# Two heads at a time in the row halves of TensorE, in the second block's two attentions of a fused two-block network

## The chip, the cores and the metric

The kernel runs on one core of one Trainium2 chip. The metric is the device time of one execution in microseconds (us), taken as the median over runs. TensorE (PE in the profile, PEld its weight loads) multiplies into PSUM, which has eight banks of 2 KB in each of 128 partitions; VectorE (DVE), ScalarE (ACT) and GpSimd (POOL) work on its results; SyncE (SP) starts the weight transfers.

## The reference, cut to what matters

One batch, 256 tokens, 1024 channels, all in float32. A first block (three mixers and a feed-forward) is followed by a second block, whose mixer has two attentions; a mixture of 32 experts follows and its weights are most of what is read from memory. Only the two attentions are changed:

```python
def hybrid_mixer(h, ...):
    z = h @ w_in                                   # fq fk fv ff dq dk dv and two gates
    log_f = log_sigmoid(ff + b_fgate)              # 8 heads
    o_a = fox_attention(fq, fk, fv, log_f)         # 8 heads of 64
    ob = diff_attention(q1, q2, k1, k2, vh, lam, slopes)   # 4 heads, two maps of 64 each, values of 128
    ...
def fox_attention(q, k, v, log_f):
    F = cumsum(log_f)
    s = q k^T * scale + F[query] - F[key]          # causal mask, softmax
    return softmax(s) v
def diff_attention(...):
    s1 = q1 k1^T * scale + bias;  s2 = q2 k2^T * scale + bias   # bias: -slope * distance, mask by chunks of 64
    return (softmax(s1) - lam * softmax(s2)) v
```

The softmax leaves F[query] out, since it is the same for a whole row.

## The kernel before, in words

Everything is one program on one core. Tokens are two tiles t of 128; a score tile is 128 queries by 128 keys for t=0 and by 256 keys for t=1, and so 384 numbers in a row for a head. In float32 a product is issued as two passes, which is why one call in the code shows as `x2` in the trace. The large projections are split into a high and a low part (`wh`/`wl`, `xT2h`/`xT2l`), and are three passes each: the tiles `acc_c` (q and k projections by `lin_chan`, 256 columns a pass) and `acc_t` (v and the gates by `lin_tok`, 512 columns a pass) are those.

The second block (`block2`) is a set of Python generators: `fk`, `fq`, `fv`, `dk`, `dq`, `dv`, `g0` to `g3` (projections and gates), `fg` (`forget`, the sums of log_f), `f0` to `f3` (`fox(b)`, heads 2b and 2b+1), `d0` to `d3` (`diff(h)`), and the projections of the outputs after them. The list `ORDER2` says in which order their pieces are written, each `yield` ending a piece; a scheduler then fixes the order of each engine's queue, by which instruction is ready when. So the small matmuls of the attentions stand between the passes of `acc_c` and `acc_t` on PE.

Names used below: `fsc` and `dsc` are the score tiles, `fptr` and `dptr` the transposed probabilities, `fPT` their copy in SBUF, `fpo` and `dpo` the outputs of the two attentions, `pF` the sums of log_f and `nFh`/`nFl` its high and low parts, `sel8` a pattern of ones and zeros that adds one row of them to all queries, `cb` constants in bf16 (the causal mask; for `dsc` distances and slopes). `attn_probs` takes the maximum of a row (`prm`, DVE), the exponential with its sum (`pr`, ACT) and a reciprocal (`prs`, DVE). At the start of the block `ptx` transposes the tokens `xt` to `xT2h`/`xT2l`, and `prb` spreads the norm's factor, which comes from `ssum`, `rmsa`, `rrms` and `dg`, over a tile.

In `fox` one head after another has its scores in one bank of the tag `mn`: for each t a product of 64 rows, two sums of 8 rows each, and the mask. In `diff` each (t, map) has a bank of `mn` of its own, one product of 64 rows and one bias matmul of 128 rows. q and k of two heads (or of two maps) lie in the partitions 0 to 63 and 64 to 127 of one tile; a product of 64 rows uses one half of the array's rows. `fpo` has its two heads in the partitions 0 to 63 and 64 to 127 of one bank, so that each matmul uses one half of the array's columns.

PSUM banks come from a pool `ps` that lives from the first block to the end of the second: three for `acc`, two for `mg`, three for `mn`. After the second block other pools take their place.

Of the kernel before, what the change touches and what calls it, by code (L numbers as in the profile page):

```python
# [18 lines left out]
P = 128  # L19
# [13 lines left out]
ORDER2 = ("fk x x fq fk fk fk fk lam fq fq fv fq fq fq x fg fg fk fv fv fv fv fv dk f1 f1 dk f2 f1 f2 f1 dq f0 "  # L33
# [133 lines left out]
def fused_kernel(ctx, tc, I, out, dbg=None):  # L167
# [28 lines left out]
    acc, mx, mg, mn = psum("acc"), psum("mx"), psum("mg"), psum("mn")  # L196
# [209 lines left out]
    with ExitStack() as st:  # L406
# [6 lines left out]
        with banks("ps", acc=3, mg=2, mn=3):  # L413
            acc(), mg()
            block1(K)
            later_inputs()
            ffn(K)
            K.st8.close()
            dump("x1", xt)
            block2(K)  # L420
            dump("x2", xt)
# [858 lines left out]
def block2(K):  # L1280
    nc, tc, I = K.nc, K.tc, K.I
    V, S, G, PE = K.V, K.S, K.G, K.PE
    C, CB, PR, idn, idb, mg, mn, acc, dump = K.C, K.CB, K.PR, K.idn, K.idb, K.mg, K.mn, K.acc, K.dump
    xt, sp, xT = K.xt, K.sp, K.x2
    with ExitStack() as st:
# [21 lines left out]
        nFh = we.tile([8, T], F32R, name="nFh")  # L1307
        nFl = we.tile([8, T], F32R, name="nFl")
        sel8 = we.tile([8, 8], F32R, name="sel8")
# [30 lines left out]
        def forget():  # L1340
# [4 lines left out]
            V.tensor_copy(sel8, idn[:8, :8])  # L1345
# [3 lines left out]
            pF = mn((8, T), name="pF")  # L1349
            PE.matmul(pF, sf[:, 0], C("UT"), start=True, stop=False)  # L1350
            PE.matmul(pF[:, P:], sf[:, 1], C("UT")[:, :P], start=False, stop=True)
            S.activation(nFh, pF, AF.Copy)
            V.tensor_tensor(nFl, pF, nFh.bitcast(F32), op=OP.subtract)
# [19 lines left out]

        def fox(b):
            po = None
            for i in range(2):
                h, hh = 2 * b + i, slice(64 * i, 64 * i + 64)
                sc = mn((P, 384), name="fsc")
                for t in range(2):
                    nk = P * (t + 1)  # L1380
                    o = sc[:, t * P:t * P + nk]
                    PE.matmul(o, fqT[hh, b, t * P:t * P + P], fkT[hh, b, :nk], start=t == 0, stop=False, skip_group_check=True)
                    PE.matmul(o, sel8[:, h:h + 1].to_broadcast([8, P]), nFh[:, :nk], start=False, stop=False, skip_group_check=True)
                    PE.matmul(o, sel8[:, h:h + 1].to_broadcast([8, P]), nFl[:, :nk], start=False, stop=False, skip_group_check=True)
                    PE.matmul(o[:, nk - P:], idb, CB("CM"), start=False, stop=t == 1, skip_group_check=True)
                yield
                ptr = mg((P, 384), name="fptr")
                for t in range(2):
                    nk = P * (t + 1)
                    pr, sm = attn_probs(K, we, sc, t * P, nk, "pr")  # L1390
                    G.tensor_scalar(pr[:, :nk], pr[:, :nk], sm, 1.0, op0=OP.mult, op1=OP.mult)
                    transpose_probs(pr, t, ptr)
                PT = we.tile([P, 384], F32, name="fPT", tag="PT2", bufs=2)
                S.activation(PT, ptr, AF.Copy)
                yield
                if not i:
                    po = mn((P, T), name="fpo")
                PE.matmul(po[hh], fv[:, 0, h * 64:h * 64 + 64], PT[:, :T], start=True, stop=False)
                PE.matmul(po[hh, P:], fv[:, 1, h * 64:h * 64 + 64], PT[:, T:], start=False, stop=True)
# [6 lines left out]
        def diff(h):  # L1406
            ptr = mg((P, 384), name="dptr")
            for t in range(2):
                nk = P * (t + 1)
                e = []  # L1410
                for i in range(2):
                    hh = slice(64 * i, 64 * i + 64)
# [80 lines left out]
        def mix(n):  # L1493
            ns = slice(n * 512, n * 512 + 512)
            y = gate[:, :, :D]
            if not ys:
                ys.append(K.Rows(y, None, "yT2", (K.s8a, K.s8a)))
# [563 lines left out]
```

## Time and profile before

| | |
|---|---|
| time, median of 3 runs | 1055.98 us (1054.99 to 1058.1) |
| the profiled execution: its time | 1054.65 us |
| its span in the trace | 1052.8 us |
| mean granted TensorE clock | 0.991 |
| PE busy | 1029.7 us (98%) |
| DVE, ACT, POOL busy | 448.4 us (43%), 290.1 us (28%), 207.1 us (20%) |
| moved by DMA | 292.57 MB, mean 278 GB/s |

The span is what the engines' records cover; 1.85 us of the execution lie outside it. The second block's part treated here runs from about 370 to 540 us in the span, and the experts from about 600 us to the end.

### The profile page before, as it was taken

What the parts mean: (1) busy time and instruction counts of PE and PEld (TensorE: products, weight loads), DVE (VectorE), ACT (ScalarE), POOL (GpSimd) and SP (SyncE); (2) the same over time, 40 slices, a digit from 0 to 9 for tenths busy, and PEclk for the clock granted to TensorE, in tenths of its full rate; (3) what the DMA queues carried; (4) which work ended last, traced back from release to release, by engine and by line L of the source; (5) the groups of instructions that cost most, each with busy time, mean ns of one, the idle gap of its engine ahead of it and who ended that gap; (6) DMA issues with size and microseconds to landing.
All of it is one profiled execution on the core that took longest, in us unless ns stands there. A gap on an engine that the chain in (4) does not pass through costs nothing. (4 is left out here: it accounts for less than half of the span.)

```text
span 1052.8 us, 16017 instructions
## 1 busy us (share of the span) xinstructions
PE 1029.7 (98%) x6373; PEld 719.0 (68%) x6373; DVE 448.4 (43%) x929; ACT 290.1 (28%) x628; POOL 207.1 (20%) x299
## 2 busy tenths in 40 slices
PE   7999999999999999999999999999999999999995
PEld 6789777988899897876788644445444555555553
DVE  4676768666555744346677411111111111111112
ACT  4554344333223453234443211110011110110012
POOL 3662262222222243332334200000000000000000
PEclk9999999999999999899999999999999999999998
DMA  9552287556555553243668899999999999999993
GB/s 347 156 156 81 78 204 275 177 193 199 185 176 188 165 178 123 100 141 128 216 244 332 321 377 422 421 421 419 420 421 421 420 419 421 419 421 420 418 390 106
DMA packets 83596, 292.57 MB, mean 278 GB/s; under 512 B 11648, under 2 KB 27840, under 8 KB 60480
## 3 DMA queue, kind: packets, MB, share of 16 engines
q1 hardware_dynamic: 82368, 289.68, 73.5%
q10 hardware_dynamic: 1152, 1.86, 0.5%
q8 instruction: 51, 0.84, 0.3%
q14 instruction: 25, 0.20, 0.1%
HBM read 289.87 MB, written 1.64 MB: 277 GB/s over the span
## 5 line engine op out<-in xcount | busy, mean ns | idle before, releaser
L1733 PE MATMUL ph<-w,xe 128*64 128x512 f32 x1024 | 224.9, 593 | 0.0
L1733 PEld LDWEIGHTS ph<-w,xe 128*64 128x64 f32 x1024 | 85.7, 137 | 128.4 <-issue 126.2
L1733 PE MATMUL po_e<-w,gT 128*64 128x512 f32 (+1 forms) x528 | 115.1, 584 | 0.7 <-ACT gT L1833 0.7
L294 DVE TENSOR_TENSOR wl<-ffn,wh 128x512 fp32r<-128x512 f32 (+1 forms) x100 | 85.2, 855 | 62.4 <-ACT wh L293 31.4
L308 POOL TENSOR_TENSOR r<-r4a,mhalf 128x2 f32<-128x2 f32 x1 | 0.7, 697 | 449.9 <-DVE r4a L306 449.9
L1733 PEld LDWEIGHTS po_e<-w,gT 128*64 128x64 f32 x528 | 39.3, 136 | 64.7 <-issue 59.6
L1749 DVE TENSOR_TENSOR oh<-cm,rk 128x256 f32<-128x256 f32 x15 | 6.4, 425 | 177.8 <-PE ppt L1733 177.8
L291 POOL TENSOR_SCALAR wh<-ffn 128x512 fp32r<-128x512 f32 (+1 forms) x50 | 44.6, 893 | 138.5 <-PE acc_c L401 61.1
L401 PE MATMUL acc_c<-xTfl,wh 128*128 128x256 f32 x256 | 70.2, 283 | 0.0
L400 PE MATMUL acc_c<-xTfh,wh 128*128 128x256 f32 x256 | 70.1, 283 | 0.0
L1817 ACT ACTIVATE pT<-ppt 128x256 fp32r<-128x256 f32 x16 | 6.1, 383 | 229.2 <-PE ppt L1733 211.1
L402 PE MATMUL acc_c<-xTfh,wl 128*128 128x256 f32 x256 | 64.6, 283 | 0.0
L1733 PEld LDWEIGHTS pgat<-oh,xp 128*128 128x128 f32 x512 | 61.0, 192 | 3.9 <-issue 2.0
L1733 PE MATMUL pgat<-oh,xp 128*128 128x128 f32 x512 | 62.9, 276 | 0.5 <-DVE oh L1749 0.5
L293 ACT ACTIVATE wh<-ffn 128x512 fp32r<-128x512 f32 (+1 forms) x50 | 37.4, 750 | 85.0 <-PE acc_c L401 42.2
L299 PE MATMUL acc<-wl,hh 128*128 128x512 f32 x128 | 50.8, 397 | 0.1
L300 PE MATMUL acc<-wh,hl 128*128 128x512 f32 x128 | 50.6, 395 | 0.0
L401 PEld LDWEIGHTS acc_c<-xTfl,wh 128*128 128x128 f32 x256 | 49.0, 192 | 0.5
L400 PEld LDWEIGHTS acc_c<-xTfh,wh 128*128 128x128 f32 x256 | 48.8, 191 | 0.4
L402 PEld LDWEIGHTS acc_c<-xTfh,wl 128*128 128x128 f32 x256 | 45.6, 191 | 0.1
L1758 DVE TENSOR_TENSOR xe<-pgat,p 128x512 f32<-128x512 f32 (+1 forms) x34 | 22.4, 660 | 48.4 <-PE pgat L1733 48.3
L299 PE MATMUL acc_t<-wl,xT2h 128*128 128x512 f32 x96 | 39.6, 412 | 0.0
(741 smaller groups left out, 2025.1 us busy)
## 6 DMA issues: line engine op xcount, KB each, us to landing
w<-in_w_dram SPq DMA_DIRECT2D x180, 1024.0 KB, 19.8
ffn<-in_w_ffn_dram SPq DMA_DIRECT2D x32, 1024.0 KB, 5.4
w_gate<-in_w_in_dram SPq DMA_DIRECT2D x8, 1024.0 KB, 5.2
w<-in_w_dram SPq DMA_DIRECT2D x16, 512.0 KB, 10.7
cmp_w<-in_cmp_w_dram SPq DMA_DIRECT2D x4, 1024.0 KB, 5.5
w_o<-in_w_o_dram SPq DMA_DIRECT2D x4, 1024.0 KB, 5.1
w<-in_w_dram SPq DMA_DIRECT2D x16, 256.0 KB, 5.8
w_in_ks<-in_w_in_dram SPq DMA_DIRECT2D x2, 1024.0 KB, 10.3
```

Source lines behind the costliest of these rows:

```text
L291: G.tensor_scalar(hi, w32, 1.0, 1.0, op0=OP.mult, op1=OP.mult)
L293: S.activation(hi, w32, AF.Copy)
L294: (G if eng == "p" else V).tensor_tensor(lo, w32, hi.bitcast(F32), op=OP.subtract)
L299: PE.matmul(o, a[0], b[1], start=False, stop=False)
L300: PE.matmul(o, a[1], b[0], start=False, stop=stop)
L400: PE.matmul(o, a[0], b[0], start=start, stop=False, skip_group_check=True)
L401: PE.matmul(o, a[0], b[1], start=False, stop=False, skip_group_check=True)
L402: PE.matmul(o, a[1], b[0], start=False, stop=stop, skip_group_check=True)
L1733: last[0] = PE.matmul(*a, **k).ins
L1749: V.tensor_tensor(o, sl, bc(rk[:, :, 2 * p_:2 * p_ + 2], (P, 2, 2, CAP), 3), op=OP.is_equal)
L1758: V.tensor_tensor(xe[:, c0:c0 + n], pg, bc(gmo[:, c0:c0 + n], (P, n, P), 2), op=OP.mult)
L1817: S.activation(pT, ppt[:, :2 * P].rearrange("p (t s) -> p t s", t=2), AF.Copy)
```

## The change

The block gets a pool of PSUM banks of its own, `ps2`, opened when the feed-forward has been written: `acc` three banks, `mg` two, `mn` one, and `m2` one double bank of two times 512 numbers a row. In `fox` and `diff` the new `products` writes for each t the products of both heads (or maps) one after the other, each to its own half of the double bank. The sums of log_f take one matmul for each head and t: `nF` holds the high part in the partitions 0 to 31 and 64 to 95 and the low part in 32 to 63 and 96 to 127, and `sel8` has its pattern four times, so that a half of 64 rows adds both parts. To fill `nF`, `pF` is 128 rows wide, from a tile `sx` with the eight columns of `sf` repeated at four places. All masks (or biases) of a pair come behind its products, then the softmax of both heads. `fpo` takes both heads for t=0 and then for t=1. `ORDER2` is written anew for the smaller number of pieces, and `yT2` takes `mg`.

```diff
@@ -30,9 +30,9 @@
           "rec z z a5 prep z a3 z z cmp pm fin rec a5 no fin o pm fin no")
 SPL2 = dict(fq="p", fk="a", fv="g", dq="g", dk=None, dv=None, g0="g", g1="a", g2="g", g3="a", pa="a", pb=None, o0=None, o1=None, o2=None)
 BK2 = dict(fq="acc", fk="acc", fv="acc", dq="acc", dk="acc", dv="acc", g0="acc", g1="acc", g2="acc", g3="acc")
-ORDER2 = ("fk x x fq fk fk fk fk lam fq fq fv fq fq fq x fg fg fk fv fv fv fv fv dk f1 f1 dk f2 f1 f2 f1 dq f0 "
-          "f0 f0 dk f2 f0 f3 f0 f2 f3 f2 f3 f1 dk dk dq dq dq dq f3 dv dq dk dv dv dv g0 dv d3 f3 d0 d0 g0 g0 "
-          "g0 g0 pa d1 g1 dv g2 d1 d1 d1 d2 d3 d2 d0 d2 d2 d3 d0 d3 g1 g1 g1 g1 sn sn g1 g2 g0 pb g2 g2 g3 g2 "
+ORDER2 = ("fk x x fq fk fk fk fk lam fq fq fv fq fq fq x fg fg fk fv fv fv fv fv dk f1 dk f1 f2 dk f1 dq f2 "
+          "f0 dk f2 f0 dk f3 dk f0 f3 dq dq dq f3 dq dv dq dk dv dv dv g0 dv dv d3 d3 d0 g0 d3 d0 g0 d1 g0 "
+          "g0 pa d0 d1 g1 d2 d1 g2 d2 d2 g1 g1 g1 g1 sn sn g1 g2 g0 pb g2 g2 g3 g2 "
           "g3 g3 g2 g3 g3 wo wo m0 m0 m0 m0 m0 m1 m1 m1 m1 g3 out m1")
 S1 = 5
 SLOTS = "wxyz01234dcbarrrrrrfegh"
@@ -193,7 +193,7 @@
         return tile_
 
 
-    acc, mx, mg, mn = psum("acc"), psum("mx"), psum("mg"), psum("mn")
+    acc, mx, mg, mn, m2 = psum("acc"), psum("mx"), psum("mg"), psum("mn"), psum("m2")
 
 
     off = {}
@@ -417,6 +417,7 @@
             ffn(K)
             K.st8.close()
             dump("x1", xt)
+        with banks("ps2", acc=3, mg=2, mn=1, m2=1):
             block2(K)
             dump("x2", xt)
         yp = ctx.enter_context(tc.tile_pool(name="psy", bufs=1, space=PSUM, reuse_waits="tile"))
@@ -1280,7 +1281,7 @@
 def block2(K):
     nc, tc, I = K.nc, K.tc, K.I
     V, S, G, PE = K.V, K.S, K.G, K.PE
-    C, CB, PR, idn, idb, mg, mn, acc, dump = K.C, K.CB, K.PR, K.idn, K.idb, K.mg, K.mn, K.acc, K.dump
+    C, CB, PR, idn, idb, mg, mn, m2, acc, dump = K.C, K.CB, K.PR, K.idn, K.idb, K.mg, K.mn, K.m2, K.acc, K.dump
     xt, sp, xT = K.xt, K.sp, K.x2
     with ExitStack() as st:
         st3 = st.enter_context(ExitStack())
@@ -1304,9 +1305,9 @@
         ob, osq = ob.rearrange("p (t h e) -> p t h e", t=2, h=4), osq.rearrange("p (k e) -> p k e", e=P)
         lq = we.tile([P, 2, 64], F32, name="lq")
         dg = we.tile([P, 2, P], F32, name="dg")
-        nFh = we.tile([8, T], F32R, name="nFh")
-        nFl = we.tile([8, T], F32R, name="nFl")
-        sel8 = we.tile([8, 8], F32R, name="sel8")
+
+        nF = we.tile([P, T], F32R, name="nF")
+        sel8 = we.tile([P, 8], F32R, name="sel8")
         rbc = we.tile([P, T], F32, name="rbc")
         prb = mn((P, T), name="prb")
         for t in range(2):
@@ -1342,15 +1343,20 @@
             lf = we.tile([P, 2, 8], F32, name="lf")
             K.lin_few(xT, PR("wff"), 8, we, lambda t, pv: V.scalar_tensor_tensor(lf[:, t], pv, r[:, t:t + 1], PR("bfg"),
                                                                                  op0=OP.mult, op1=OP.add), "dg")
-            V.tensor_copy(sel8, idn[:8, :8])
+            with nc.allow_low_precision(reason="zeros and ones"):
+                V.tensor_reduce(sel8, idn.rearrange("p (g j) -> p j g", g=4)[:, :8], axis=AX.X, op=OP.add)
+            sx = we.tile([P, 2, 4, 32], F32, name="sx")
+            G.memset(sx, 0.0)
             yield
             V.tensor_scalar(lf, lf, -1.0, None, op0=OP.mult)
             sf = softplus(V, S, we, lf, [P, 2, 8], "fsp")
-            pF = mn((8, T), name="pF")
-            PE.matmul(pF, sf[:, 0], C("UT"), start=True, stop=False)
-            PE.matmul(pF[:, P:], sf[:, 1], C("UT")[:, :P], start=False, stop=True)
-            S.activation(nFh, pF, AF.Copy)
-            V.tensor_tensor(nFl, pF, nFh.bitcast(F32), op=OP.subtract)
+            G.tensor_copy(sx[:, :, :, :8], bc(sf, (P, 2, 4, 8), 2))
+            pF = mn((P, T), name="pF")
+            PE.matmul(pF, sx[:, 0].rearrange("p g j -> p (g j)"), C("UT"), start=True, stop=False)
+            PE.matmul(pF[:, P:], sx[:, 1].rearrange("p g j -> p (g j)"), C("UT")[:, :P], start=False, stop=True)
+            S.activation(nF, pF, AF.Copy)
+            for q in (32, 96):
+                V.tensor_tensor(nF[q:q + 32], pF[q:q + 32], nF[q:q + 32].bitcast(F32), op=OP.subtract)
 
         def lam():
             pq = PR("lq").rearrange("p (a b) -> p a b", a=4)
@@ -1371,32 +1377,46 @@
 
         oaT = (wk.tile([P, 4, T], F32R, name="oaTh"), wk.tile([P, 4, T], F32R, name="oaTl"))
 
+        def products(sc, qT, kT, b):
+
+            for t in range(2):
+                nk = P * (t + 1)
+                for i in range(2):
+                    hh = slice(64 * i, 64 * i + 64)
+                    PE.matmul(sc[i][:, t * P:t * P + nk], qT[hh, b, t * P:t * P + P], kT[hh, b, :nk],
+                              start=t == 0, stop=False, skip_group_check=True)
+
         def fox(b):
-            po = None
+            sc = m2((P, 2, 512), name="fsc")
+            sc = [sc[:, i] for i in range(2)]
+            products(sc, fqT, fkT, b)
+            for t in range(2):
+                nk = P * (t + 1)
+                for i in range(2):
+                    hh = slice(64 * i, 64 * i + 64)
+                    PE.matmul(sc[i][:, t * P:t * P + nk], sel8[hh, 2 * b + i:2 * b + i + 1].to_broadcast([64, P]), nF[hh, :nk],
+                              start=False, stop=False, skip_group_check=True)
             for i in range(2):
-                h, hh = 2 * b + i, slice(64 * i, 64 * i + 64)
-                sc = mn((P, 384), name="fsc")
                 for t in range(2):
-                    nk = P * (t + 1)
-                    o = sc[:, t * P:t * P + nk]
-                    PE.matmul(o, fqT[hh, b, t * P:t * P + P], fkT[hh, b, :nk], start=t == 0, stop=False, skip_group_check=True)
-                    PE.matmul(o, sel8[:, h:h + 1].to_broadcast([8, P]), nFh[:, :nk], start=False, stop=False, skip_group_check=True)
-                    PE.matmul(o, sel8[:, h:h + 1].to_broadcast([8, P]), nFl[:, :nk], start=False, stop=False, skip_group_check=True)
-                    PE.matmul(o[:, nk - P:], idb, CB("CM"), start=False, stop=t == 1, skip_group_check=True)
-                yield
+                    PE.matmul(sc[i][:, 2 * t * P:2 * t * P + P], idb, CB("CM"), start=False, stop=t == 1, skip_group_check=True)
+            yield
+            PT = []
+            for i in range(2):
                 ptr = mg((P, 384), name="fptr")
                 for t in range(2):
                     nk = P * (t + 1)
-                    pr, sm = attn_probs(K, we, sc, t * P, nk, "pr")
+                    pr, sm = attn_probs(K, we, sc[i], t * P, nk, "pr")
                     G.tensor_scalar(pr[:, :nk], pr[:, :nk], sm, 1.0, op0=OP.mult, op1=OP.mult)
                     transpose_probs(pr, t, ptr)
-                PT = we.tile([P, 384], F32, name="fPT", tag="PT2", bufs=2)
-                S.activation(PT, ptr, AF.Copy)
-                yield
-                if not i:
-                    po = mn((P, T), name="fpo")
-                PE.matmul(po[hh], fv[:, 0, h * 64:h * 64 + 64], PT[:, :T], start=True, stop=False)
-                PE.matmul(po[hh, P:], fv[:, 1, h * 64:h * 64 + 64], PT[:, T:], start=False, stop=True)
+                PT.append(we.tile([P, 384], F32, name="fPT", tag="PT2", bufs=2))
+                S.activation(PT[i], ptr, AF.Copy)
+            yield
+            po = mn((P, T), name="fpo")
+            for t in range(2):
+                for i in (1, 0):
+                    h = 2 * b + i
+                    PE.matmul(po[64 * i:64 * i + 64, t * P:], fv[:, t, h * 64:h * 64 + 64], PT[i][:, t * T:T + t * P],
+                              start=t == 0, stop=t == 1)
             S.activation(oaT[0][:, b], po, AF.Copy)
             V.tensor_tensor(oaT[1][:, b], po, oaT[0][:, b].bitcast(F32), op=OP.subtract)
 
@@ -1404,18 +1424,18 @@
         sli = CB("SLI")
 
         def diff(h):
+            sc = m2((P, 2, 512), name="dsc")
+            sc = [sc[:, i] for i in range(2)]
+            products(sc, dqT, dkT, h)
+            for i in range(2):
+                for t in range(2):
+                    PE.matmul(sc[i][:, t * P:2 * t * P + P], sli[:, h * P:h * P + P], CB(f"DIST{t}"),
+                              start=False, stop=t == 1, skip_group_check=True)
+            yield
             ptr = mg((P, 384), name="dptr")
             for t in range(2):
                 nk = P * (t + 1)
-                e = []
-                for i in range(2):
-                    hh = slice(64 * i, 64 * i + 64)
-                    sc = mn((P, T), name="dsc")
-                    PE.matmul(sc[:, :nk], dqT[hh, h, t * P:t * P + P], dkT[hh, h, :nk], start=True, stop=False)
-                    PE.matmul(sc[:, :nk], sli[:, h * P:h * P + P], CB(f"DIST{t}"), start=False, stop=True)
-                    e.append(attn_probs(K, we, sc, 0, nk, "pr"))
-                yield
-                (p1, s1), (p2, s2) = e
+                (p1, s1), (p2, s2) = [attn_probs(K, we, sc[i], t * P, nk, "pr") for i in range(2)]
                 V.tensor_tensor(s2, s2, nlam, op=OP.mult)
                 G.tensor_scalar(p1[:, :nk], p1[:, :nk], s1, 1.0, op0=OP.mult, op1=OP.mult)
                 V.scalar_tensor_tensor(p1[:, :nk], p2[:, :nk], s2, p1[:, :nk], op0=OP.mult, op1=OP.add)
@@ -1494,7 +1514,7 @@
             ns = slice(n * 512, n * 512 + 512)
             y = gate[:, :, :D]
             if not ys:
-                ys.append(K.Rows(y, None, "yT2", (K.s8a, K.s8a)))
+                ys.append(K.Rows(y, None, "yT2", (K.s8a, K.s8a), mg))
             yT = ys[0]
 
             def eva(t, pv):
```

On PE, at the border between the feed-forward and the second block, the queue before reads as follows (`acc` with a number and `hh`, `hl` is the feed-forward's last product, `acc_c<-xT2...` the projection `fk`; `c` with a number the identity):

```order
L299 MATMUL acc_2370<-wl,hh 128x512
L300 MATMUL acc_2370<-wh,hl 128x512
L400 MATMUL acc_c<-xT2h,wh 128x256 x2
L401 MATMUL acc_c<-xT2l,wh 128x256
L402 MATMUL acc_c<-xT2h,wl 128x256
L400 MATMUL acc_c<-xT2h,wh 128x256
L401 MATMUL acc_c<-xT2l,wh 128x256
L402 MATMUL acc_c<-xT2h,wl 128x256
L401 MATMUL acc_c<-xT2l,wh 128x256
L402 MATMUL acc_c<-xT2h,wl 128x256
```

and 17 rows on, still between rows of `acc_c`:

```order
L325 MATMUL ptx<-c_69,xt 128x128 x2
L402 MATMUL acc_c<-xT2h,wl 128x256
L400 MATMUL acc_c<-xT2h,wh 128x256
L401 MATMUL acc_c<-xT2l,wh 128x256
L402 MATMUL acc_c<-xT2h,wl 128x256
L325 MATMUL ptx<-c_69,xt 128x128 x6
L400 MATMUL acc_c<-xT2h,wh 128x256
```

Now it reads:

```order
L299 MATMUL acc_2370<-wl,hh 128x512
L300 MATMUL acc_2370<-wh,hl 128x512
L325 MATMUL ptx<-c_69,xt 128x128 x8
L1315 MATMUL prb<-dg,c_69 128x128 x2
L400 MATMUL acc_c<-xT2h,wh 128x256
L401 MATMUL acc_c<-xT2l,wh 128x256
L402 MATMUL acc_c<-xT2h,wl 128x256
L400 MATMUL acc_c<-xT2h,wh 128x256
```

The eight transposes and both matmuls of `prb` stand ahead of the first matmul of `fk`; before, 24 rows of `fk` stood ahead of the first transpose and more ahead of `prb`.

On PE, the scores of one head of the forgetting attention before (the head after it has the same rows, three transposes later):

```order
L1382 MATMUL fsc<-att_4233 128x128
L1383 MATMUL fsc<-nFh,sel_4244 128x128
L1384 MATMUL fsc<-nFl,sel_4244 128x128
L1385 LDWEIGHTS cb
L1385 MATMUL fsc<-cb 128x128
L1382 MATMUL fsc<-att_4233 128x256
L1383 MATMUL fsc<-nFh,sel_4244 128x256
L1384 MATMUL fsc<-nFl,sel_4244 128x256
L1385 LDWEIGHTS cb
L1385 MATMUL fsc<-cb 128x128
L1369 MATMUL fptr<-c_69,pr 128x128 x3
```

and the scores of two heads now, between rows of `acc_c`:

```order
L1386 MATMUL fsc<-att_4237 128x128 x2
L1386 MATMUL fsc<-att_4237 128x256 x2
L1397 MATMUL fsc<-nF,sel_4247 128x128 x2
L1397 MATMUL fsc<-nF,sel_4247 128x256 x2
L1401 LDWEIGHTS cb
L1401 MATMUL fsc<-cb 128x128
L1401 LDWEIGHTS cb
L1401 MATMUL fsc<-cb 128x128
L1401 LDWEIGHTS cb
L1401 MATMUL fsc<-cb 128x128
L1401 LDWEIGHTS cb
L1401 MATMUL fsc<-cb 128x128
```

Sixteen products, sums and masks of two heads have become twelve, and those of one shape stand together.

On PE, in the differential attention before (a place with three score tiles for 256 keys, between rows of `acc_t`):

```order
L300 MATMUL acc_t<-wh,xT2l 128x512
L1414 MATMUL dsc<-att_4235,att_4234 128x256
L1415 LDWEIGHTS cb
L1415 MATMUL dsc<-cb 128x256
L1414 MATMUL dsc<-att_4235,att_4234 128x256
L1415 LDWEIGHTS cb
L1415 MATMUL dsc<-cb 128x256
L1414 MATMUL dsc<-att_4235,att_4234 128x256
L1415 LDWEIGHTS cb
L1415 MATMUL dsc<-cb 128x256
L298 MATMUL acc_t<-wh,xT2h 128x512 x2
```

and a whole head now:

```order
L298 MATMUL acc_t<-wh,xT2h 128x512 x2
L1386 MATMUL dsc<-att_4239,att_4238 128x128 x2
L1386 MATMUL dsc<-att_4239,att_4238 128x256 x2
L1432 LDWEIGHTS cb
L1432 MATMUL dsc<-cb 128x128
L1432 LDWEIGHTS cb
L1432 MATMUL dsc<-cb 128x256
L1432 LDWEIGHTS cb
L1432 MATMUL dsc<-cb 128x128
L1432 LDWEIGHTS cb
L1432 MATMUL dsc<-cb 128x256
L299 MATMUL acc_t<-wl,xT2h 128x512
```

The four products of a head stand together, two and two on the two halves, and its four bias matmuls behind them.

## Rows read from the trace of the kernel before

**Rows 1.** Stretches: length, busy us PE, PEld, DVE, ACT, POOL; clock, DMA share, GB/s
```profile
423.80:430.60 6.80, 6.80 (x29) 5.90 (x29) 2.70 (x9) 2.14 (x8) 2.27 (x4) 0.50 0.01 2
490.00:500.00 10.00, 10.00 (x51) 7.79 (x51) 6.18 (x14) 8.14 (x15) 0.48 (x1) 1.00 0.41 129
630.00:700.00 70.00, 70.00 (x376) 33.69 (x373) 11.73 (x28) 6.80 (x12) 0.00 (x0) 1.00 1.01 421
```

**Rows 2.** SP's waits, 340 to 700 us: total us, times, longest us
```profile
SPq L1583 <- PE ph L1733: 40.0, 13, 8.5
```

**Rows 3.** PE in order of time, one head of fox (--timeline)
```profile
start us, us, engine line op out<-in xcount [idle before <-releaser]
419.61 0.65 PE L1398 MATMUL fpo<-fPT,att 128*64 128x256 f32 x2
420.09 0.38 PE L1399 MATMUL fpo<-fPT,att 128*64 128x128 f32 x2
420.41 0.48 PE L1382 MATMUL fsc<-att 64*128 64x128 f32 x2
420.82 0.32 PE L1383 MATMUL fsc<-nFh,sel 8*128 8x128 f32 x1
...
421.19 0.23 PE L1385 MATMUL fsc<-cb 128*128 128x128 bf16 x1
421.34 0.70 PE L1382 MATMUL fsc<-att 64*128 64x256 f32 x2
421.97 0.38 PE L1383 MATMUL fsc<-nFh,sel 8*128 8x256 f32 x1
...
422.40 0.23 PE L1385 MATMUL fsc<-cb 128*128 128x128 bf16 x1
422.46 0.49 PE L1369 MATMUL fptr<-c,pr 128*128 128x128 f32 x3
```

**Rows 4.** The same view in the first block, two stretches with products of 64 rows
```profile
69.14 1.13 PE L761 MATMUL sc<-kT,qT 64*128 64x512 f32 x4
70.21 0.39 PE L763 MATMUL sc<-cb 128*128 128x256 bf16 x2
...
134.06 1.12 PE L761 MATMUL sc<-kT,qT 64*128 64x512 f32 x2
135.11 0.28 PE L763 MATMUL sc<-cb 128*128 128x256 bf16 x1
```

**Rows 5.** The same view, a product of diff among passes of the projections
```profile
468.26 0.63 PE L298 MATMUL acc_t<-wh,xT2h 128*128 128x512 f32 x2
468.82 0.48 PE L1414 MATMUL dsc<-att,att 64*128 64x128 f32 x2
469.24 0.50 PE L299 MATMUL acc_t<-wl,xT2h 128*128 128x512 f32 x1
469.58 0.39 PE L300 MATMUL acc_t<-wh,xT2l 128*128 128x512 f32 x1
469.81 0.39 PE L299 MATMUL acc_t<-wl,xT2h 128*128 128x512 f32 x1
```

**Rows 6.** The same view, an expert's products in column halves
```profile
701.74 1.51 PE L1733 MATMUL po_e<-w,gT 128*64 128x512 f32 x6
```

**Rows 7.** Their group on the page (the costliest groups)
```profile
L1733 PE MATMUL po_e<-w,gT 128*64 128x512 f32 (+1 forms) x528 | 115.1, 584 | 0.7 <-ACT gT L1833 0.7
```

**Rows 8.** All engines in order of time, the border to the second block
```profile
370.67 0.40 PE L400 MATMUL acc_c<-xT2h,wh 128*128 128x256 f32 x2
...
374.04 0.71 POOL L308 TENSOR_TENSOR rrms<-rmsa,mhalf 128x2 f32<-128x2 f32 x1 [6.82 <-DVE rmsa L306]
374.41 0.82 PE L325 MATMUL ptx<-c,xt 128*128 128x128 f32 x6
374.83 0.48 DVE L1313 TENSOR_SCALAR dg<-c,rrms 128x128 f32<-128x128 f32 x2
374.98 0.36 PE L400 MATMUL acc_c<-xT2h,wh 128*128 128x256 f32 x1
```

**Rows 9.** ACT in order of time, the end of that head's softmax
```profile
424.45 0.47 ACT L1275 ACTIVATE pr<-fsc,prm 128x256 f32<-128x256 f32 x1 [0.61 <-DVE prm L1272]
```

## Prediction

> **What bounds the kernel now.** I read first the busy time in stretches. From 490 to 500 us, among the attentions, PE is busy for all 10.00 us at the full clock, while ACT has 8.14, DVE 6.18 and the DMA engines 0.41 of their time [rows 1]; of the engines only PE has no room. From 630 us on it is the DMA engines that are full (1.01, at 421 GB/s) [rows 1]. So a second question comes before the sum: does time saved before 540 us reach the end? The waits of SP's queue answer it. SP starts the experts' weights, and what holds it back is above all PE: 40.0 us in 13 waits for the experts' own `ph` products, which free the buffers [rows 2]. The stream can't run ahead of the program; if PE comes to the experts earlier, the stream starts earlier. I take a saved microsecond at its full worth, and keep the opposite as a rival.
>
> Then I read PE in order of time, from start to start, since matmuls overlap and their lengths don't add up. One head of `fox` runs from 420.41 to 422.46 us with nothing between, 2.05 us [rows 3]. Its parts: the product for 128 keys 0.41 us, two sums 0.37, the mask 0.15, the product for 256 keys 0.63, two sums 0.43, the mask 0.06.
>
> **What a pair costs.** The first block has the answer in its own trace. Products of 64 rows and 512 columns, x4, which are two calls, take 69.14 to 70.21 us, 1.07 us; a single call, x2, takes 134.06 to 135.11 us, 1.05 us [rows 4]. Two calls for the price of one can only be two halves at work together. The change issues its products the same way, so I count those of a pair as those of one head.
>
> *Fox, scores.* Before: eight heads at 2.05 us, 16.4 us. After, for a pair: products 0.41 + 0.63 = 1.04 us; one sum in place of two for each t, both heads at once, 0.19 + 0.21 = 0.40; four masks at 0.06, since they now follow each other, 0.24. That is 1.68 us, 6.7 us for four pairs: **-9.7 us**. From above: if halves follow one another the pair takes 2.08 + 0.80, and masks at 0.15 make 0.60, 3.48 us in all, and 2.5 us are saved. From below: 128 more columns cost 0.63 - 0.41 = 0.22 us, so 0.41 holds 0.19 us that isn't streaming; paid once and not twice, the products of a pair cost 0.85, and another 0.8 us go in `fox` and 0.8 in `diff`. I take the middle bound, which changes least against the rows.
>
> *Diff, scores.* Four heads of two maps, each with products of 0.42 us for 128 keys (468.82 to 469.24 us [rows 5]) and 0.63 for 256, 8.4 us. After: half, **-4.2 us**; nothing if the halves don't overlap. The bias matmuls stay as many as they were and cost the same.
>
> *Outputs.* `fpo` takes 0.48 us (419.61 to 420.09) and 0.32 us (to 420.41) a head [rows 3], 6.4 us for eight. Two column halves do run together: in the experts six products begin and end within 1.51 us [rows 6], though one has a mean of 0.584 us [rows 7], so that six in single file would take far more. After, a pair for the price of a head: **-3.2 us**, from below 0.
>
> *Neighbours.* Two passes of the projection before a product take 468.26 to 468.82 us, 0.56 us, where a pass among its own takes 0.23 (469.58 to 469.81), so 0.10 us are lost on the way in; the pass after the product takes 0.34 (469.24 to 469.58), 0.11 lost on the way out [rows 5]. In the listing of PE's queue the ways in fall from 23 to 14, the ways out from 12 to 7: 9 x 0.10 + 5 x 0.11, **-1.5 us**.
>
> A rule bears on this and on the products. The Trainium skill, TensorEngine Tiling (Array Packing), Key Properties, has it that changing the tiling mode, and not merely the tile, drains TensorE. The rows agree that a switch costs about 0.1 us, but don't show whether it is a drain. By that rule products of two heads behind each other would pay only at the first, and the sum would be about 1.6 us lower, as in the bound from below.
>
> *The clock.* From 423.80 to 430.60 us the granted clock is 0.50 (1.2 GHz), 6.8 us in which PE is busy throughout [rows 1]. Ahead of it PE ran, from 419.61 us, only half-array outputs, scores and masks [rows 3], two heads in a row. Work of 6.8 us at half speed takes 3.4 at full. After the change the same two heads' scores are 1.7 us long and have projections on both sides in the listing: **-3.4 us**, or 0 if it falls at another place.
>
> Together -22.0 us.
>
> **What is added.** *The border.* The new pool's banks are the old pool's, so `fk` can't begin while the old pool is in use. Before, its matmuls begin at 370.67 us and fill PE while the norm is worked out [rows 8]. In the listing they now stand behind eight `ptx` and both `prb`. `prb` needs `dg`, which was written at 374.83 + 0.48 = 375.31 us [rows 8]; about 375.5 us for the first `fk`, 4.8 us later. What PE does meanwhile it need not do later: six transposes took 374.41 to 374.98 us [rows 8], 0.095 each, so eight and the four passes of `prb` are 1.1 us, and three interruptions of `fk` go, 0.3 us. **+3.4 us**; 2.5 if ACT, which has no weights to split now between the norm's two halves, brings `dg` sooner, 5 if the banks come free later. Behind `fk` on PE stand `fq` and all else of the block, so nothing makes it good.
>
> *The clock after it.* PE would be all but idle for some 3 us there. The only price in the rows is that fall, 3.4 us [rows 1]; I give it an even chance, **+1.7 us** (0 to 3.4).
>
> *Forget.* A copy on POOL now stands between `sf` and `pF`. A small POOL operation takes 0.71 us (`rrms` [rows 8]); projections cover part of it, and without them all of it would show on PE. **+0.4 us** (0 to 0.7). `pF` 128 rows wide takes PE no longer, as it has as many columns; two subtractions in place of one are DVE's.
>
> *One double bank.* A pair's products wait until the exponentials of the pair before have been read out of `m2`. For the head above the exponential of its 256 keys ends at 424.45 + 0.47 = 424.92 us [rows 9], 2.5 us after its last mask began at 422.40 [rows 3]; a second head on the same engines adds 1 to 2 us, so 3.5 to 4.5 us. In `diff` 25 to 31 passes of the projection stand between the pairs, 5.8 to 7.1 us at 0.23 [rows 5]. It fits where ACT is free, and ACT is at 8.14 of 10 in the densest stretch [rows 1]. **+1.0 us** (0 to 4).
>
> The rest costs nothing: `yT2` in `mg` and a single `mn` bank come where tiles follow each other at a distance, covered by projections; without that cover a handover is an ACT read of about 0.5 us [rows 9].
>
> Added +6.5 us. **Sum:** -22.0 + 6.5 = -15.5 us on the profiled 1054.65 us, 1039.2 us. The median of the runs shown lies 1.3 us above that execution; I forecast **1040 us**.
>
> **Rivals.**
> 1. *The gain stops at the feeders.* If PE gets through the attentions faster than ACT and DVE can serve it, or the weight stream hides part, half of the 15.5 us is lost: about 1048 us. For it: ACT at 8.14 of 10 in one stretch. Against: PE never waited for them there.
> 2. *Halves in single file.* The Trainium skill, TensorEngine Tiling (Array Packing), Gotcha 1, says that different row tiles can't write one PSUM bank at the same time; here each half has a bank of its own, and no run shows the other case. As a mechanism of this kernel, if halves don't overlap: -2.5 - 0 - 0 - 1.5 - 3.4 + 6.5 = -0.9 us, about 1055 us. Against: the 1.07 us of the first block.
> 3. *Slower.* PE waits at `m2`, in front of each of eight pairs, for the last exponential of the pair before. All projections queued behind wait too. It decides from 15.5 / 8 = 1.9 us a pair above the 1.0 us I count in all; at 2.5 us a pair it is about 1059 us. Against: 5.8 us of projections between pairs; for it: every wait of ACT and DVE for other work lengthens the chain.
> 4. *Better.* No fall of the clock at the border, and products at the bound from below: 1.7 + 1.6 us lower, and nothing lost at `m2`, about 1035.5 us.
>
> **How the numbers follow.** The forecast 0.58 (1036 to 1045 us, by its terms' bounds), rival 1 0.14, rival 2 0.06, rival 3 0.08, rival 4 0.14. What a measurement of this kernel can tell from no change is about 0.3%, 3.2 us. Faster than that: the first, 1 and 4, and a third of 2, 0.88. Rival 3 is slower but for a small part, 0.07; the rest, 0.05, is the same. The range 1031 to 1051 us holds the forecast and rivals 1 and 4, and leaves out 2 and 3 and their like.
>
> **What would show it.** Right: the products of a pair of heads start within a few hundredths of a microsecond of each other and the pair is through in 1.7 us; `fpo` of a pair takes 0.8; no stretch at 0.50 near 424 us; PE has a gap of about 3 us at the border; the experts' first product comes some 15 us earlier and the end with it. Wrong: waits of PE for ACT or DVE before `fsc` or `dsc`, a clock below 1.00 in several stretches of the attentions, a border gap much over 5 us, or an end that doesn't follow the start of the experts.

## The result, and the profile after

The changed kernel's median was 1041.32 us (1038.41 to 1046.26, four runs) against 1056.45 us before (1054.99 to 1058.1, four runs). The ratio is 0.9867, with a 95% interval of 0.9844 to 0.9891. The forecast was 1040 us, in a range of 1031 to 1051. The four runs lie in two groups, 1038.41 and 1038.64 us at a granted clock of 0.995, and 1044.0 and 1046.26 us at 0.988 and 0.985. The profiled execution is the one of 1044.0 us, with a span of 1041.8 us.

In the changed kernel's trace, PE in order of time, first a pair of heads of `fox` and its outputs, then a head of `diff` (columns as in [rows 3]):

```profile
441.90 0.93 PE L1386 MATMUL fsc<-att 64*128 64x128 f32 x8
442.47 0.58 PE L1397 MATMUL fsc<-nF,sel 64*128 64x128 f32 x4
442.98 0.40 PE L1401 MATMUL fsc<-cb 128*128 128x128 bf16 x4
443.22 0.39 PE L1375 MATMUL fptr<-c,pr 128*128 128x128 f32 x2
...
446.48 0.87 PE L1418 MATMUL fpo<-fPT,att 128*64 128x256 f32 x8
447.28 0.38 PE L400 MATMUL acc_c<-xT2h,wh 128*128 128x256 f32 x1
...
467.24 0.93 PE L1386 MATMUL dsc<-att,att 64*128 64x128 f32 x8
468.10 0.50 PE L1432 MATMUL dsc<-cb 128*128 128x128 bf16 x4
468.36 0.48 PE L299 MATMUL acc_t<-wl,xT2h 128*128 128x512 f32 x1
```

Two heads' scores go from 441.90 to 443.22 us, 1.32 us, where one head took 2.05 [rows 3] (the form printed is that of a group's first row; each group holds both widths). The outputs of both heads take 446.48 to 447.28, 0.80 us. Four products and four biases of `diff` take 467.24 to 468.36, 1.12 us. The eight passes of a pair's products take 0.57 us from start to start where the sums follow at once (441.90 to 442.47) and 0.86 where work of full height follows (467.24 to 468.10).

The border, in the same view of the same kernel:

```profile
372.04 0.40 PE L300 MATMUL acc<-wh,hl 128*128 128x512 f32 x1
372.88 0.44 PE L325 MATMUL ptx<-c,xt 128*128 128x128 f32 x2 [0.45 <-DVE xt L644]
373.54 0.87 PE L325 MATMUL ptx<-c,xt 128*128 128x128 f32 x6 [0.22 <-DVE xt L644]
376.03 1.22 PE L1315 MATMUL prb<-dg,c 128*128 128x128 f32 x4 [1.62 <-DVE dg L1314]
376.91 0.56 PE L400 MATMUL acc_c<-xT2h,wh 128*128 128x256 f32 x1
```

The first pass of `fk` starts 4.87 us after the last of the feed-forward; before, it started right behind it [rows 8]. A gap, with waits for `xt` and `dg`, is what had been expected.

Busy time in stretches of the changed kernel (columns as in [rows 1]):

```profile
370.00:384.00 14.00, 11.71 (x63) 10.45 (x63) 7.54 (x22) 6.69 (x18) 0.71 (x1) 0.76 0.45 141
400.00:470.00 70.00, 69.96 (x491) 58.15 (x490) 40.62 (x105) 27.59 (x74) 33.03 (x49) 1.00 0.48 160
500.00:510.00 10.00, 8.37 (x35) 5.72 (x34) 7.36 (x10) 1.00 (x2) 6.99 (x7) 1.00 0.58 210
620.00:700.00 80.00, 80.00 (x430) 38.24 (x428) 14.08 (x31) 8.61 (x15) 0.00 (x0) 1.00 1.01 420
```

In this execution the clock did fall behind the border (0.76 on average over 14 us). From 400 to 470 us, where the kernel before had its slow stretch [rows 1], it stays at 1.00. There is a new hole in PE from 500 to 510 us. The experts run as before at the full rate of the DMA engines.

PE's time can be added up from the start of each instruction to the start of the next, by the tile written, from the last feed-forward pass to the experts' first product. In us, before, for the changed kernel's profile, and for a second profile of it (the first experiment); of the tiles left out none differs by more than 0.3:

```
            before   changed   changed, second profile
fsc          17.43      5.87      5.88
dsc           9.79      4.40      4.40
fpo           6.36      3.56      3.56
acc_c        50.26     50.25     47.87
acc_t       117.47    118.19    118.22
ptx           2.12      4.57      4.57
acc, last     0.23      0.84      0.84
prb           0.28      0.87      0.47
pobT          0.71      1.34      1.33
plg           3.26      4.01      4.01
y             3.94      5.50      3.83
all         224.90    212.29    207.85
first experts' product to the end of the span
            457.5     457.5     457.5
```

From the experts on the program takes as long as before: every microsecond gained ahead of them reached the end. The two profiles of the changed kernel are 5.4 us apart. Of this, 2.8 us are the slow stretch behind the border (`acc_c` and `prb`), 1.7 us another one near 577 to 580 us (`y`), and 0.9 us arose in the first block.

### The profile page after: what moved, and what is told of

Its sections match the earlier page's. It is cut to its first block, busy times and chain, and to the rows that moved or that the text cites. A ratio compares the mean times of both kernels' runs of the same rounds, so it can differ in the third digit from the quotient of the medians.

```text
span 1041.8 us, 15989 instructions
## 1 busy us (share of the span) xinstructions
PE 1014.0 (97%) x6357; PEld 711.8 (68%) x6357; DVE 449.0 (43%) x930; ACT 291.2 (28%) x628; POOL 211.2 (20%) x301
## 6 DMA issues: line engine op xcount, KB each, us to landing
w<-in_w_dram SPq DMA_DIRECT2D x16, 512.0 KB, 11.6
```

## Experiments

**The changed kernel again.** No edit. 

> The changed kernel once more, for its spread and for the clock. If the two groups of its times (1038.4 and 1038.6 against 1044.0 and 1046.3 us) come from falls of TensorE's clock, the granted clock of a run orders them: about 0.995 near 1038 us, about 0.986 near 1045 us, and a profile near 1038 us has no stretch at 0.50 near 376 us. If they come from something else, times of one clock differ by as much.

Median 1038.51 us (1037.8 to 1043.46, six runs), ratio 0.9834 (0.9803 to 0.9865). Five runs at a clock of 0.995 lie between 1037.8 and 1038.64 us, the one at 0.988 at 1043.46. So the spread goes with the clock. The profile, at 0.995, has no slow stretch behind the border though it has the same gap:

```profile
370.00:390.00 20.00, 17.72 (x142) 16.10 (x141) 10.34 (x28) 9.39 (x21) 4.59 (x4) 1.00 0.50 169
```

**The border alone.** The kernel before, with a new pool of the same size as its old one:

```diff
+        with banks("ps2", acc=3, mg=2, mn=3):
             block2(K)
```

> The kernel before, with the new pool alone (the same number of banks as its old one). Theory: the border alone costs 3 to 3.5 us, and up to 3.4 more by the clock: 1059 to 1063 us. Rival: the gap is made good later, because something else than PE sets the end: 1056 us, within 1 us of the kernel before.

Median 1060.75 us (1054.53 to 1066.39, twelve runs), ratio 1.0046 (1.0023 to 1.007): slower, as the theory had it. In its trace `ptx` takes 4.57 us, the last feed-forward pass 0.84 and `prb` 0.74, which is 3.5 us more than before, and PE waits 1.6 us for `dg`. No fall of the clock follows the gap here either. The medians are 6.0 us apart (1054.74 us for the kernel before in the same series), so the border's rows leave 2.5 us open. In the profile two slow stretches in the first block, near 34 to 37 and 88 to 102 us, make that block longer; whether that is it in the median, too, stays open.

**Products head by head.** Only the loops of `products` change places:

```diff
-            for t in range(2):
-                nk = P * (t + 1)
-                for i in range(2):
+            for i in range(2):
+                for t in range(2):
+                    nk = P * (t + 1)
```

> The changed kernel with the products written head by head (t inside), so that two products of one half follow each other before those of the other half. Theory: the gain of the scores is the overlap of neighbours on different halves; products of a pair then take 1.2 to 1.3 us in place of 0.86, 8 pairs, 3 to 4 us more than the changed kernel: about 1044.5 us. Rival: the gain comes from fewer changes between shapes, not from overlap: the same as the changed kernel within 1 us.

Median 1038.7 us (1037.77 to 1040.64): no change. The time is the rival's, but not for the rival's reason. The trace, PE in order of time:

```profile
405.02 0.93 PE L1386 MATMUL fsc<-att 64*128 64x128 f32 x8
405.88 0.50 PE L299 MATMUL acc_t<-wl,xT2h 128*128 128x512 f32 x1
```

All eight passes are through in 0.86 us. From start to start they come in couples 13 ns apart: 405.021 and 405.034 us with 128 columns, 405.346 and 405.359 with 256. In the queue the second head's first pass stands behind four passes of the first, two of 128 columns and two of 256. A record doesn't name its half, but the widths tell: all four passes of 128 columns start before the first of 256. So the second head's passes start ahead of passes that precede them in the queue. The halves do work at once, and needn't be neighbours for it.

**Heads apart.** Now work of full height stands between the heads of a pair, the double bank and all else unchanged:

```diff
-            products(sc, fqT, fkT, b)
-            for t in range(2):
-                nk = P * (t + 1)
-                for i in range(2):
+            for i in range(2):
+                products(sc, fqT, fkT, b, i)
+                for t in range(2):
+                    nk = P * (t + 1)
                     hh = slice(64 * i, 64 * i + 64)
...
-            for i in range(2):
                 for t in range(2):
                     PE.matmul(sc[i][:, 2 * t * P:2 * t * P + P], idb, CB("CM"), start=False, stop=t == 1, skip_group_check=True)
```

and the same in `diff`. 

> The changed kernel with the two heads (or maps) of a pair one after the other: products, sums and the masks of full height of the first, then those of the second; the double bank and everything else stay. Theory: what is gained is the two halves at work together, and work of full height between them ends that. The products of a head then take about the 0.85 us that a pair takes now, 8 pairs, 6.8 us more; the sums 0.4 us more for 4 pairs, and one more way in and out for each pair, 1.6 us together: 10 us above the changed kernel, about 1048 us. Rival: the gain comes from fewer and longer runs of small matmuls; then the products of a pair stay near 0.9 us and the time within 2 us of the changed kernel.

Median 1044.99 us (1044.3 to 1045.65), 6.5 us above the changed kernel: the direction of the theory, two thirds of its size. `fsc` is 9.97 us and `dsc` 8.26, that is 4.1 and 3.9 us more. One head of `fox` in its trace, then two maps of `diff`:

```profile
417.49 0.92 PE L1385 MATMUL fsc<-att 64*128 64x128 f32 x4
418.06 0.57 PE L1396 MATMUL fsc<-nF,sel 64*128 64x128 f32 x2
418.57 0.29 PE L1399 MATMUL fsc<-cb 128*128 128x128 bf16 x2
418.66 0.36 PE L402 MATMUL acc_c<-xT2h,wl 128*128 128x256 f32 x1
...
467.76 0.92 PE L1385 MATMUL dsc<-att,att 64*128 64x128 f32 x4
468.61 0.34 PE L1430 MATMUL dsc<-cb 128*128 128x128 bf16 x2
468.88 0.92 PE L1385 MATMUL dsc<-att,att 64*128 64x128 f32 x4
```

A head alone takes 1.17 us (417.49 to 418.66), not 2.05. Its products take 0.57 us with the sums behind them (which then take 0.51 in place of 0.43) and 0.85 with work of full height behind (467.76 to 468.61), not 1.04, though no other half helps. That is also what a pair's products take in the changed kernel, 0.57 and 0.86: at work together, the second half costs next to nothing. What differs from [rows 3] is the order: all products, then all sums, then all masks, where before each t had its product, sums and mask. So both parts of the explanation are shown. Grouping by shape, with the merged sums, is the larger share in `fox`; the halves at once add 4 us there and most of the gain in `diff`. The first share is what is left between this run and the kernel before; the new `ORDER2` and the sums of 64 rows in place of 8 are in it too, and no run takes them apart.

**Sums apart.** High and low part in matmuls of their own, each with a pattern `sel8[p]` that is zero at the other part's rows:

```diff
-                    PE.matmul(sc[i][:, t * P:t * P + nk], sel8[hh, 2 * b + i:2 * b + i + 1].to_broadcast([64, P]), nF[hh, :nk],
...
+                    for p in range(2):
+                        PE.matmul(sc[i][:, t * P:t * P + nk], sel8[p][hh, 2 * b + i:2 * b + i + 1].to_broadcast([64, P]), nF[hh, :nk],
...
```

> The changed kernel with the high and the low part of the sums in matmuls of their own again, still on halves of 64 rows. Theory: a pair's sums go from 0.42 to about 0.8 us, four pairs: 1.5 us above the changed kernel, near 1040 us, which the profile can show and the time hardly. Rival: sums hide between their neighbours, no difference in the profile.

Median 1038.56 us (1037.45 to 1041.5). `fsc` is 7.08 us, 1.2 more, near the theory; the time can't tell it. From the last feed-forward pass to the experts the profile is 0.8 us longer than the changed kernel's second one, but its experts happen to be 1.8 us shorter.

**Outputs by head.**

```diff
-            for t in range(2):
-                for i in (1, 0):
+            for i in (1, 0):
+                for t in range(2):
```

> The changed kernel with the outputs written head by head (both t of one column half, then of the other). As the halves' products kept their pace when written head by head, no neighbour is needed: fpo stays near 3.6 us in all and the time at 1038.5 us. Rival: column halves need their partner next in the queue; fpo takes 5 us or more.

Median 1039.5 us (1038.11 to 1041.15), and `fpo` is 3.58 us: the theory. Its trace shows a pair of column halves through in 0.81 us, as in the changed kernel:

```profile
434.36 0.88 PE L1418 MATMUL fpo<-fPT,att 128*64 128x256 f32 x8
435.17 0.39 PE L401 MATMUL acc_c<-xT2l,wh 128*128 128x256 f32 x1
```

**No pool of its own, no double bank.** A pair takes two of the old pool's three `mn` banks:

```diff
-        with banks("ps2", acc=3, mg=2, mn=1, m2=1):
             block2(K)
...
-            sc = m2((P, 2, 512), name="fsc")
-            sc = [sc[:, i] for i in range(2)]
+            sc = [mn((P, 384), name="fsc") for i in range(2)]
```

and the same in `diff`. 

> The change without its own pool of banks: the block stays in the first block's pool, and a pair takes two of the three mn banks in place of the double bank. Theory: the border gap goes (first fk pass within 0.3 us of the last feed-forward pass in place of 4.9 us after it), and 3.2 us with it (4.6 less 1.4 us of work moved into the gap); where the clock fell after the gap, 3 us more. 3 to 6 us below the changed kernel's median, about 1036 us, and no slow stretch near 376 us. Rival: pF, fpo, dpo and pobT now rotate through the same three banks as the scores, and PE waits for them: no better than the changed kernel, 1041 us or more, with waits of PE before fsc or dsc.

Median 1042.86 us (1042.06 to 1043.95), 4.4 us above the changed kernel's repeat: the rival's time, though not by its waits. The gap is gone, `ptx` back at 2.12 us. But `fsc` is 8.33 us, `dsc` 6.76 and `dptr` 2.90 (0.65 in the changed kernel), with waits of PE of 0.7 us before `dptr` and of 1.4 us for ACT's `wh`, but none before `fsc` or `dsc`. Its trace shows a pair that came apart, PE in order of time:

```profile
410.51 0.49 PE L1385 MATMUL fsc<-att 64*128 64x128 f32 x2
410.93 0.74 PE L298 MATMUL acc_t<-wh,xT2h 128*128 128x512 f32 x2
411.59 0.70 PE L1385 MATMUL fsc<-att 64*128 64x256 f32 x2
412.22 0.50 PE L299 MATMUL acc_t<-wl,xT2h 128*128 128x512 f32 x1
```

Projections stand between a head and its partner. That points to the two single banks, of which one comes free before the other, where the double bank frees both at once; `fsc` and `dsc` together take 4.8 us more in this run. Pool and double bank went together here: a run with a pool of its own and two single banks was not made.

**Only `mn` changes its banks.** `acc` and `mg` stay in one pool through both blocks, and the tag is looked up in the enclosing pools:

```diff
-        with banks("ps", acc=3, mg=2, mn=3):
+        with banks("ps", acc=3, mg=2):
+            with banks("psn", mn=3):
...
-        with banks("ps2", acc=3, mg=2, mn=1, m2=1):
-            block2(K)
+            with banks("ps2", mn=1, m2=1):
+                block2(K)
```

> The changed kernel with the banks of acc and mg in one pool through both blocks, and only those of mn given to the new pool with its double bank. Theory: fk starts right behind the feed-forward (0.23 us after its last pass, not 4.5), pairs stay together (products of a pair 0.86 us, fsc about 5.9 us in all), and 3 to 3.5 us go: about 1035.3 us. Rival: the time stays at 1038.5 us, because the gap was made good later or other waits of equal length come.

Median 1033.37 us (1032.67 to 1034.61, six runs), ratio 0.9794 (0.9759 to 0.9829): 5.1 us below the changed kernel's repeat. It is the best version of the study, better than both kernels. Its border, PE in order of time:

```profile
370.41 0.40 PE L300 MATMUL acc<-wh,hl 128*128 128x512 f32 x1
370.64 0.40 PE L400 MATMUL acc_c<-xT2h,wh 128*128 128x256 f32 x2
370.88 0.28 PE L401 MATMUL acc_c<-xT2l,wh 128*128 128x256 f32 x1
```

`fsc` (5.80) and `dsc` (4.40) keep their gain. From the last feed-forward pass to the experts PE takes 203.19 us, 4.66 less than in the changed kernel's second profile: 3.25 at the border (`ptx`, `acc`, `prb`), 0.74 in `plg`, 0.43 in `acc_t` and 0.36 in `fpo`. Why `plg` gains is not settled.

**The same, with another splitter.** `g0="a"` in place of `"g"` in `SPL2`. 

> The kernel in which acc lives on, with the weights of the first gate split by ACT in place of POOL (SPL2, g0). Theory: the two waits of PE for wl near the end of the attentions, 1.5 us, come from POOL, which works on the norm of the differential output then while ACT is idle; they go, and 1 to 1.5 us with them: about 1032 us. Rival: ACT has the exponentials of the last pairs to do, and PE waits for them or for wh instead: 1033.4 us or more.

Median 1033.63 us (1032.97 to 1035.71): no gain. PE's wait for `wl` is still 1.5 us in two pieces. But the edit missed the place, and the run doesn't test its theory: what went to ACT are the eight splits between 455 and 470 us. The weights that PE waits for, at 494.82 and 500.30 us, belong to a later gate, whose splits stayed on POOL, behind POOL's work for the norm:

```profile
490.59 1.89 POOL L1458 TENSOR_TENSOR att<-att 128x1024 f32<-128x1024 f32 x1 [1.67 <-DVE att L1452]
492.45 1.78 POOL L291 TENSOR_SCALAR wh<-w_gate 128x512 fp32r<-128x512 f32 x3
```

In the changed kernel's second profile the longer of the same two waits ends at 499.76 us with

```profile
497.45 1.22 DVE L1459 TENSOR_REDUCE oss<-att 128x8 f32<-128x1024 f32 x1 [2.01 <-POOL att L1457]
498.58 1.73 DVE L294 TENSOR_TENSOR wl<-w_gate,wh 128x512 fp32r<-128x512 f32 x2
499.76 0.50 PE L299 MATMUL acc_t<-wl,xT2h 128*128 128x512 f32 x1 [0.97 <-DVE wl L294]
```

DVE's reduction for the norm of the `diff` output stands ahead of the split in its queue, and had itself waited 2.01 us for POOL's product. That points to the norm's chain through POOL and DVE; no run took it away.

**The kernel before, its clock.** Two profiles, no edit. 

> The kernel before once more, for its clock. If its scores in long runs of small matmuls make the clock fall, a stretch at 0.50 shows again between 400 and 470 us, though not at the same place; if the fall at 424 us was chance, like those of the first block, which come and go, there is none.

> The kernel before a third time, for the same question: a stretch at 0.50 between 400 and 470 us in each of three profiles, or in one or two of them, or in none but the first.

The times were 1057.31 and 1057.43 us. Busy time in stretches, first of the one and then of the other:

```profile
400.00:470.00 70.00, 70.00 (x401) 54.63 (x399) 31.77 (x78) 20.09 (x54) 22.32 (x36) 0.95 0.36 120
```

```profile
400.00:470.00 70.00, 70.00 (x391) 53.74 (x390) 30.24 (x74) 20.01 (x54) 21.64 (x36) 0.93 0.34 111
```

The fall came in each, near 427 us in the one, near 412 and again near 430 us in the other, and in the border experiment as well (0.95 over the same 70 us). In the changed kernel's two profiles the same 70 us are at 1.00. What such a stretch costs can be read from the passes of `acc_c`. In the first profile of the kernel before the slow stretch holds

```profile
426.11 0.42 PE L401 MATMUL acc_c<-xT2l,wh 128*128 128x256 f32 x1
...
430.37 0.39 PE L400 MATMUL acc_c<-xT2h,wh 128*128 128x256 f32 x1
```

with nothing but passes of `acc_c` between, twenty from start to start, 0.213 us each; at full clock in the same profile a pass takes 0.117 (22 of them from 416.71 to 419.29). So 0.45 of the slow time is lost, and a stretch of 6.8 us costs about 3.0 us.

## Why the prediction was right, point by point

The sum foresaw -15.5 us on a profiled execution. The second profile of the changed kernel lies 16.0 us under the profiled 1054.65 us (1038.64 us). The stretch of the block gives -17.05 us by start to start; the block starts 0.7 us later in that profile, where the first block's slow stretch fell at 158 us and not at 99, and 0.3 us more lie outside the span.

That the sum came so near is in part luck, since its errors cancel. The scores gained 2.2 us more than forecast and the clock after the border cost nothing in that profile, where 1.7 us had been put down; the neighbours, the outputs and the clock gave 1.3 us less, and waits that had not been named cost 2.9 us, where 1.4 had been put down for others. It is luck too that the median of the four runs lies 1.3 us from the forecast: two of them are near 1038.5 us and two at 1044 and 1046. The terms:

- *Fox, scores: -9.7.* Measured 17.43 to 5.87 us, -11.6; with the 0.8 us of it that the slow stretch had caused, which the clock's term holds, -10.7. The size was right, and nearest to the bound from below: a pair's products take 0.86 us where work of full height follows (0.85 was that bound), and 0.57 where the sums follow. The reason was right in part. Of the 9.7 us the working puts 5.8 on halves at once (products and sums of two heads for one) and 3.9 on the merged sums and the masks, and nothing on the products' place in the queue. By the run with the heads apart the halves are 4.1 us; the merged sums and the grouping by shape are the other 6.6.
- *Diff, scores: -4.2.* Measured -5.4, of which 3.9 by the halves; the other 1.5, by grouping, was left out of the sum.
- *Outputs: -3.2.* Measured -2.8. Three pairs take 0.80 us as forecast; one was split in the queue. Where all are whole, as in the version with `acc` living on, it is -3.2.
- *Neighbours: -1.5.* Mis-sized. `acc_c` and `acc_t` together fall by 1.6 us (167.73 to 166.09), but 2.2 of that is the clock (3.0 less the 0.8 in `fsc`), against which 1.5 us of new waits for `wl` stand: about 1.0 us is left for the neighbours.
- *The clock: -3.4.* Right that it goes; its price is about 3.0, since a pass at 0.50 takes 1.8 times as long and not twice. Four of four profiles with the old scores have the fall between 410 and 435 us, none of eight with the pairs in a double bank. One came at 491 us in the version without it. That the long run of small matmuls is the cause is not shown beyond this.
- *The border: +3.4.* Measured 3.25 (2.45 in `ptx`, 0.61 in the last feed-forward pass, 0.19 in `prb`).
- *The clock after the border: +1.7.* The chance was mis-sized, and the price a little: of seven profiles with the gap one has the fall, the changed kernel's first, where `acc_c` is 2.4 us and `prb` 0.4 us dearer than in the second, 2.8 us and not 3.4. The gap alone doesn't make the clock fall each time.
- *Forget: +0.4, double bank: +1.0.* Neither showed: PE waits nowhere for `pF`, `fsc` or `dsc`. In their place stand the 1.5 us for `wl`, 0.6 in `pobT` and 0.75 in `plg`, which I had not named. The first is what rival 1 described, at a fifth of its size.

Rival 2 priced halves in single file at about 1055 us. The run with the heads apart, which is that case for the scores (the outputs, 3.2 us, still go two at a time), shows 1045: the arithmetic had left out what grouping by shape is worth by itself. Of the drain rule (the Trainium skill, TensorEngine Tiling (Array Packing), Key Properties) this is the trace's side: 0.57 us for a head's four passes in a row against 1.04 when each t had sums and a mask behind its product, and no price for going from half to half. It agrees with the rule, but doesn't show that a drain is what a change of shape costs. The sum by that rule, 1.6 us lower, was the nearer of the two in the scores.

## What to carry to other kernels

When small matmuls of several shapes alternate on a full TensorE, put those of one shape together first, and then let two halves of the array work at once; here the first, with the merged sums, was worth 6.6 us in `fox` and 1.5 in `diff`, the second 6.5 us of the time. Matmuls that belong together should get their PSUM in one piece; in the one run with two single banks the scheduler pulled them apart. A new pool over all of the old banks put 4.87 us between two projections here, in place of 0.23: hand over only the banks that change their use.

## What the runs showed of the hardware that was not expected

Two row halves find each other across the queue: in the run with products head by head, the second half's first pass began 13 ns after the first half's first, although four passes of the first half stood ahead of it. Column halves did the same (`fpo` in 0.81 us head by head). Where work of full height stood between, nothing was pulled forward (the second map's products at 468.88 us, behind the biases of the first at 468.61). A pass of `acc_c` at 0.50 took 1.8 times as long as at full clock, 0.213 us for 0.117. And the spread of this kernel's times goes with the clock: five runs at 0.995 within 0.9 us, one at 0.988 some 5 us later.
